# Softmax blocks transposed as they are: normalising attention outputs by row sums, and joining the two maps of differential attention, in a two-layer step

## The chip, the core and the metric

The kernel runs on one core of a Trainium2 chip. The metric is the device time of one execution in microseconds (us); less is better. TensorE is PE in the profile (its weight loads are PEld), VectorE is DVE, ScalarE is ACT, GpSimd is POOL, and SyncE, which issues many of the DMAs, is SP.

## What is computed

One inference step of a two-layer backbone on 128 prompt tokens and 512 sample tokens, model width 1024. Layer 0 mixes tokens by grouped-query attention (A, 8 heads) and by retention (B); layer 1 by differential attention (C, 4 heads, two maps each, values 128 wide) and by windowed attention (D, 8 heads, with a sink logit). After each mixer comes a channel mixer with 16384 single-neuron experts. The lines that matter here, shortened:

```python
# A and the prompt's D: softmax over keys, then the values
s = einsum('bhgqd,bhkd->bhgqk', qb, k) * scale        # D puts a sink logit in front
p = softmax(s, axis=-1)
o = einsum('bhgqk,bhkd->bhgqd', p, v)
# C: two softmax maps, one subtracted from the other
p = softmax(einsum('bhcqd,bhckd->bhcqk', qb, k) * d ** -0.5, axis=-1)
a = p[:, :, 0] - lam * p[:, :, 1]
o = einsum('bhqk,bhkv->bhqv', a, v)
c_out = rmsnorm(o, subln) * (1.0 - lam_init)
# D on sample tokens: sink, 128 context keys and a band |i-j| <= 128
p = softmax(concatenate([s_sink, s_ctx, s_band], axis=-1), axis=-1)
```

## The kernel before, in words

The activations lie transposed, features on the partitions and tokens along the free axis. The queries are taken in blocks of 128. For the sample tokens there are 640 keys (128 context, 512 own) in A and C, and three or four key blocks of 128 in D. The sample stream works in halves of two query blocks (`halves`, L756).

One softmax block is `soft_block` (L698): PE writes scores to a PSUM bank of tag `S`, DVE takes the row maximum (L713) and scales it to a bias (L716), ACT takes the exponential into the SBUF tile `P` with its row sum `rs` (L722), and DVE takes the reciprocal (L730). `win_block` (L1063) is the same for the windowed blocks, with the sink added to the sum (L1090) and the reciprocal at L1092. `P` has two buffers.

The value product needs the probabilities with keys on the partitions. Before, PE transposes and normalises at once: `diag` (L733) has DVE multiply the 128x128 identity by the reciprocals, the matrix `dg`, and `pT` (L742) multiplies each 128x128 block of `P` by `dg` in an ordinary matmul. For C (`attn_c`, L982) there are two such matrices, the second also multiplied by minus lambda (L739), and the two products add up in PSUM, so that the join of the maps costs PE two matmuls in each block. D does the same at L1037 and L1038. ACT then copies the result to SBUF (`PT`) and PE multiplies it by the values (L777, L1003, L1051, L1058).

```python
P, r = self.soft_block(...)                       # L771
self.pT([(P, self.diag(r))], nkt, pt[...])        # L772
nc.tensor.matmul(T[:, ...], P[:, o:o + 128], dg, start=i == 0, stop=i == len(parts) - 1)   # L752
```

The transposes of other tiles go through `transpose` (L316), a PE transpose against the identity. `head_bcast` (L488) spreads a per-token column over the partitions, one small matmul for each 128 tokens and head half.

What sets the order: `weave` (L235) interleaves the sample mixer with the prompt stream, with the weights of layer 1's modulation, and with the gather task (`gather_tile`, L1276). That task brings expert rows of 128x1024 by indirect DMA on POOL's queue (L1291) into eight buffers, and DVE works each up in one instruction (L1304 or L1308). The yields in the generators carry costs, and a scheduler then places every instruction on its engine by times that it reckons itself; each engine works in the order so made. PSUM in the mixers is four tags: `mm` and `S` with two buffers each, `tr` and `acc` with one. The projections (`chunk`, L554, matmuls at L474) write to `mm`, and so do rotary permutations (L501), broadcasts and the second half of `pT`. The prompt's layer 1 runs beside layer 0's dense experts, where every bank it takes is one bank, `pm`.

## Time and profile before

| | |
|---|---|
| time, median of 3 runs (range) | 4066.35 us (4053.7 to 4073.78) |
| the profiled execution's own time | 4054.7 us |
| its span in the trace | 4052.9 us |
| PE busy | 3686.1 us (91%) |
| PE weight loads busy | 3096.5 us (76%) |
| DVE busy | 3258.2 us (80%) |
| ACT busy | 1643.5 us (41%) |
| POOL busy | 1572.4 us (39%) |

Read it as an average over stages. The sample mixer of layer 0 lies at 305 to 608 us, that of layer 1 at 2255 to 2585 us; the rest is routing and dense experts, which the change does not touch. The share of an engine over the whole span says little about these two stretches, so they are read by themselves. A PE instruction's duration in the trace covers its way through the array; instructions follow one another faster than they last, so the cost of one in a row is the length of a run of them divided by their number.

### The profile page before, as it was taken

To read this page: it belongs to the slowest core of one execution; us is meant where nothing else is said; L and a number is where in the kernel's file an instruction comes from. 1 tells how busy PE (TensorE), PEld (TensorE's weight loads), DVE (VectorE), ACT (ScalarE), POOL (GpSimd) and SP (SyncE) were. 2 spreads that over 40 slices of the span, in tenths; PEclk is the share of its full clock that TensorE was granted. 3 is DMA by queue.
4 is the path that set the end of the run, shared out by engine and by line. 5 is a ranking of instruction groups with operands and counts; after the bars stand their busy time and mean duration, and the time that the engine had idled before them with its cause. 6 is when DMAs were issued, how large, how long until landed. Compare 5 with 4: busy or idle time off the path is not lost. (4 is left out here: it accounts for less than half of the span.)

```text
span 4052.9 us, 57181 instructions
## 1 busy us (share of the span) xinstructions
PE 3686.1 (91%) x19986; PEld 3096.5 (76%) x19986; DVE 3258.2 (80%) x6546; ACT 1643.5 (41%) x2971; POOL 1572.4 (39%) x1136
## 2 busy tenths in 40 slices
PE   7889888989985999999998888988977989999998
PEld 3775555889974887889886666677977878888887
DVE  3248788999998766878898888899999867777777
ACT  3223333335676333433333333333376743333333
POOL 1004655221344343433455666532142233443442
PEclk9999999999985999999998999999988989999999
DMA  8556887766878888999898677776677899998996
GB/s 324 175 176 231 320 293 274 247 230 214 286 261 306 307 325 328 349 338 352 305 315 288 238 241 257 246 249 234 215 257 246 290 341 322 342 331 302 317 312 217
DMA packets 441024, 1134.89 MB, mean 280 GB/s; under 512 B 40608, under 2 KB 191312, under 8 KB 434464
## 3 DMA queue, kind: packets, MB, share of 16 engines
q0 software_dynamic: 147904, 537.26, 37.9%
q1 hardware_dynamic: 251408, 506.28, 35.5%
q10 hardware_dynamic: 41424, 87.71, 5.9%
q8 instruction: 157, 2.57, 0.2%
q14 instruction: 131, 1.07, 0.1%
HBM read 1045.10 MB, written 85.98 MB: 279 GB/s over the span
## 5 line engine op out<-in xcount | busy, mean ns | idle before, releaser
L1291 POOL DMA_INDIRECT row<-v,xi x512 | 772.5, 1509 | 1218.9 <-DVE acc L1308 837.8
L1291 POOL DMA_INDIRECT row<-u,xi x512 | 690.8, 1349 | 793.0 <-DVE row L1304 566.5
L1400 PE MATMUL mm<-hhi,uhi 128*128 128x384 f32 x2048 | 702.4, 343 | 31.6 <-ACT uhi L1388 31.5
L1400 PE MATMUL mm<-hhi,ulo 128*128 128x384 f32 x2048 | 702.0, 344 | 27.2 <-DVE ulo L1389 27.1
L1400 PE MATMUL mm<-hlo,uhi 128*128 128x384 f32 x2048 | 697.5, 341 | 0.9 <-DVE hlo L448 0.9
L1304 DVE SCALAR_TENSOR_TENSOR row<-hn,row 128x1024 f32<-128x1024 f32 x512 | 629.2, 1255 | 27.5 <-DMA row<-u,xi 19.5
L1308 DVE SCALAR_TENSOR_TENSOR acc<-row,gw,acc 128x1024 f32<-128x1024 f32 x508 | 648.1, 1276 | 2.1
L1388 ACT CAST uhi<-u 128x1024 fp32r<-128x1024 f32 x256 | 269.7, 1053 | 535.8 <-PE mm L1400 241.3
L1423 PE MATMUL d<-vlo,Whi 128*128 128x512 f32 x1536 | 481.6, 394 | 2.1 <-DVE vlo L1464 2.0
L1423 PE MATMUL d<-vhi,Wlo 128*128 128x512 f32 x1536 | 476.4, 391 | 0.0
L1423 PE MATMUL d<-vhi,Whi 128*128 128x512 f32 x1536 | 433.3, 395 | 3.3 <-ACT vhi L1463 3.2
L1389 DVE TENSOR_TENSOR ulo<-u,uhi 128x1024 fp32r<-128x1024 f32 x256 | 311.7, 1217 | 153.8 <-ACT uhi L1388 150.8
L1400 PEld LDWEIGHTS mm<-hhi,uhi 128*128 128x128 f32 x2048 | 392.9, 192 | 45.0 <-ACT uhi L1388 38.4
L1400 PEld LDWEIGHTS mm<-hhi,ulo 128*128 128x128 f32 x2048 | 392.2, 192 | 38.6 <-DVE ulo L1389 35.4
L1400 PEld LDWEIGHTS mm<-hlo,uhi 128*128 128x128 f32 x2048 | 391.6, 191 | 6.8 <-DVE hlo L448 1.3
L1423 PEld LDWEIGHTS d<-vhi,Wlo 128*128 128x128 f32 x1536 | 288.6, 188 | 61.5
L1423 PEld LDWEIGHTS d<-vhi,Whi 128*128 128x128 f32 x1536 | 285.9, 189 | 58.5 <-ACT vhi L1463 4.7
L1423 PEld LDWEIGHTS d<-vlo,Whi 128*128 128x128 f32 x1536 | 285.8, 188 | 57.9 <-DVE vlo L1464 3.7
L1464 DVE TENSOR_TENSOR vlo<-v,vhi 128x1024 fp32r<-128x1024 f32 x256 | 311.3, 1217 | 20.2 <-ACT vhi L1463 20.1
L1471 ACT CAST Whi<-W 128x384 fp32r<-128x384 f32 x256 | 131.1, 513 | 392.8 <-PE d L1423 284.5
L1463 ACT CAST vhi<-v 128x1024 fp32r<-128x1024 f32 x256 | 268.7, 1050 | 49.3 <-DMA v<-v 32.6
L474 PE MATMUL mm<-hhi,whi 128*128 128x512 f32 x624 | 254.0, 408 | 20.5 <-ACT whi L463 6.5
(460 smaller groups left out, 6025.2 us busy)
## 6 DMA issues: line engine op xcount, KB each, us to landing
u<-ut SPq DMA_DIRECT2D x256, 512.0 KB, 5.1
v<-v SPq DMA_DIRECT2D x256, 512.0 KB, 5.9
Gd<-gst ACTq DMA_DIRECT2D x48, 1024.0 KB, 7.6
G<-Gd SPq DMA_DIRECT2D x64, 768.0 KB, 8.6
w<-win SPq DMA_DIRECT2D x80, 512.0 KB, 5.2
w<-wq SPq DMA_DIRECT2D x64, 512.0 KB, 4.7
Ad<-gpre ACTq DMA_DIRECT2D x152, 192.0 KB, 3.6
pre<-Ad SPq DMA_DIRECT2D x152, 192.0 KB, 6.1
```

Of the source, the lines that this page charges most:

```text
L474: nc.tensor.matmul(ps[:, :st.T], wp[a][:, k], h[b][:, k], start=(n == 0), stop=(n == 23))
L1291: nc.gpsimd.indirect_dma_start(out=r, out_offset=None, in_=self.A[f"{'uv'[n // 128]}{l}"], in_offset=bass.IndirectOffsetOnAxis(ap=xi[:, s: ...
L1304: nc.vector.scalar_tensor_tensor(r, hn, 1.0, r, op0=ALU.mult, op1=ALU.mult, accum_out=a[:, s:s + 1])
L1308: nc.vector.scalar_tensor_tensor(acc, r, w[:, s:s + 1], acc, op0=ALU.mult, op1=ALU.add)
L1388: nc.scalar.copy(hi, u)
L1389: nc.vector.tensor_tensor(lo, u, hi, op=ALU.subtract)
L1400: nc.tensor.matmul(ps[:, :ND], u[a][:, k], h[b][:, k, :ND], start=n == 0, stop=n == 23)
L1423: nc.tensor.matmul(acc[t][hf], a[:, ts], b[:, hf * 512:(hf + 1) * 512], start=(i == 0 and n == 0), stop=(i == 127 and n == 2))
L1463: nc.scalar.copy(vhi, v)
L1464: nc.vector.tensor_tensor(vlo, v, vhi, op=ALU.subtract)
L1471: nc.scalar.copy(whi, w)
```

## The change

Nothing is divided before the transpose any more. `soft_block` and `win_block` write the reciprocal into a column that the caller gives; `diag` is gone; `pT` and the code in D transpose `P` itself by `transpose`. In A and D the reciprocals of a chunk of two heads are gathered in a tile `ra`, and after the value product `normalise` spreads them by `head_bcast` into a `mm` bank (8 small matmuls for the sample, 2 for the prompt) and has DVE multiply the chunk of the output. In C the two unnormalised maps are joined on DVE: a factor `f` = (row sum 0) x (reciprocal 1) x (minus lambda), then P0 + f x P1 over the whole row; one transpose per block is left. The remaining factor, the reciprocal of row sum 0 (`cr`), is put into the root mean square that follows: the sums of squares are multiplied twice by `cr`, and the result once.

```diff
-    def soft_block(self, lhsT, rhs, nk, masks=None, sink=None, scale=0.125):
+    def soft_block(self, lhsT, rhs, nk, rout, masks=None, sink=None, scale=0.125):
...
-        r = self.wk.tile([128, 1], F32, tag="rr", name="rr", bufs=6)
-        nc.vector.reciprocal(r, rs)
-        return P, r
-
-    def diag(self, r, extra=None):
...
+        nc.vector.reciprocal(rout, rs)
+        return P, rs
+
+    def normalise(self, st, y, ra):
+
+        pb = self.bank("mm")
+        self.head_bcast(pb, ra, 0, st, 2)
+        self.nc.vector.tensor_tensor(y, y, pb[:, :st.T], op=ALU.mult)
...
-                for i, (P, dg) in enumerate(parts):
-                    nc.tensor.matmul(T[:, j * 128:(j + 1) * 128], P[:, o:o + 128], dg,
-                                     start=i == 0, stop=i == len(parts) - 1)
+                self.transpose(T[:, j * 128:(j + 1) * 128], P[:, o:o + 128])
...
         nc.scalar.copy(st.mo[:, cch], O[:, :st.T])
+        self.normalise(st, st.mo[:, cch], ra)
...
                 if cc == 3:
+                    for _ in range(2):
+                        nc.vector.tensor_tensor(st.hv, st.hv, st.cr, op=ALU.mult)
                     r = self.rsq(st.hv, 4 * st.nt)
+                    nc.vector.tensor_tensor(r, r, st.cr, op=ALU.mult)
...
-                    self.pT([(P0, self.diag(r0)), (P1, self.diag(r1, c["nlam"]))], nkt, pt[:, :, n * 128:(n + 1) * 128])
+                P0, s0 = self.soft_block(qs, st.ck[:, 0], st.nk, st.cr[:, hd * st.nt + i:hd * st.nt + i + 1])
+                r1 = self.wk.tile([128, 1], F32, tag="rr", name="rr", bufs=6)
+                P1, _ = self.soft_block(qs, st.ck[:, 1], st.nk, r1)
+
+                f = self.wk.tile([128, 1], F32, tag="rf", name="rf", bufs=6)
+                nc.vector.tensor_scalar(f, s0, r1, c["nlam"], op0=ALU.mult, op1=ALU.mult)
+                nc.vector.scalar_tensor_tensor(P0, P1, f, P0, op0=ALU.mult, op1=ALU.add)
+                self.pT(P0, nkt, pt[:, :, n * 128:(n + 1) * 128])
...
-                        nc.tensor.matmul(T2[:, jj * 128:(jj + 1) * 128], P[:, jj * 128:(jj + 1) * 128], dg,
-                                         start=True, stop=True)
+                        self.transpose(T2[:, jj * 128:(jj + 1) * 128], P[:, jj * 128:(jj + 1) * 128])
...
         nc.scalar.copy(st.mo[:, 4 + cch], O[:, :T])
+        self.normalise(st, st.mo[:, 4 + cch], ra)
```

Counted over the whole program, PE loses 456 matmuls against `dg` (320 of them on the sample in layer 0's A and layer 1's C counted with both maps, 112 in the sample's D, 24 on the prompt) and gains 372 transposes and 80 broadcast matmuls. An ordinary matmul of this type shows in the trace as two PE instructions, a transpose as one. DVE loses 120 products with the identity and gains 20 joins, 20 factors, 16 output products and 6 small products.

The order moves too, since the scheduler places instructions anew. Three places follow.

DVE, layer 1, sample, one query block of C (`mx` is the row maximum, `nm` the bias, `rr` and `cr` reciprocals, `row` a gathered expert row). Before:

```order
L713 TENSOR_REDUCE mx<-S 128x1 x2
L716 TENSOR_SCALAR nm<-mx 128x1 x2
L730 RECIPROCAL rr<-rs 128x1
L737 TENSOR_SCALAR dg<-c_ident,rr 128x128
L730 RECIPROCAL rr<-rs 128x1
L739 TENSOR_SCALAR dg<-c_ident,rr,lams 128x128
L1304 SCALAR_TENSOR_TENSOR row,ga<-hn,row 128x1024 x2
```

and with the change:

```order
L711 TENSOR_REDUCE mx<-S 128x1 x2
L714 TENSOR_SCALAR nm<-mx 128x1 x2
L727 RECIPROCAL cr<-rs 128x1
L727 RECIPROCAL rr<-rs 128x1
L1001 TENSOR_SCALAR rf<-rs,rr,lams 128x1
L1002 SCALAR_TENSOR_TENSOR P<-P,rf 128x640
L1308 SCALAR_TENSOR_TENSOR row,ga<-hn,row 128x1024 x2
```

The place of the two small matrices is taken by a factor and a product over 640 columns; the same two gathered rows follow.

PE, the same part of the program (`S` scores, `tr` and `mm` the banks of the transposes, `PTc` the transposed block, `cvs` the values). Before:

```order
L704 MATMUL S<-cks,cqs 128x320 x2
L752 MATMUL tr<-dg,P 128x128
L752 MATMUL mm<-dg,P 128x128
L704 MATMUL S<-cks,cqs 128x320 x2
L752 MATMUL tr<-dg,P 128x128 x5
L752 MATMUL mm<-dg,P 128x128 x3
L1003 MATMUL acc<-PTc,cvs 128x256 x5
```

and with the change:

```order
L702 MATMUL S<-cks,cqs 128x320 x4
L316 MATMUL tr<-c_ident,P 128x128 x3
L316 MATMUL mm<-c_ident,P 128x128 x2
L1007 MATMUL acc<-PTc,cvs 128x256 x5
```

Ten products for a query block become five transposes, and the scores of both maps of the next block stand ahead of them.

PE, layer 1, sample, the end of one head's D (`PTd` is D's transposed block, `vs` its values, `vsb`, `whi` and `hhi` belong to the projections of the next head, `ra` are the gathered reciprocals). Before:

```order
L1038 MATMUL tr<-dg,P 128x128 x3
L474 MATMUL mm<-hhi,whi 128x512
L474 MATMUL mm<-hlo,whi 128x512
L474 MATMUL mm<-hhi,wlo 128x512
L474 MATMUL mm<-hhi,whi 128x512
L474 MATMUL mm<-hlo,whi 128x512
L474 MATMUL mm<-hhi,wlo 128x512
L318 MATMUL mm<-c_ident,vsb 128x128 x4
L704 MATMUL S<-cks,cqs 128x320 x4
L1051 MATMUL acc<-PTd,vs 64x256
L1058 MATMUL acc<-PTd,vs 64x128
```

and with the change:

```order
L492 MATMUL mm<-c_ident,ra 64x128 x2
L1055 MATMUL acc<-PTd,vs 64x256
L1062 MATMUL acc<-PTd,vs 64x128
L316 MATMUL tr<-c_ident,P 128x128 x4
L1062 MATMUL acc<-PTd,vs 64x256 x2
L316 MATMUL tr<-c_ident,P 128x128 x3
L492 MATMUL mm<-c_ident,ra 64x128
L1055 MATMUL acc<-PTd,vs 64x256
L1062 MATMUL acc<-PTd,vs 64x128
L1062 MATMUL acc<-PTd,vs 64x256 x2
L499 MATMUL mm<-y,c_perm 128x512
L472 MATMUL mm<-hhi,whi 128x512
```

Before, all 96 projection matmuls of the next head stand between D's blocks, and the next head's first scores ahead of its last product. With the change 48 of the 96 and the rotary permutation stand behind D. The first broadcast of `ra` stands near D's beginning, so its `mm` bank is taken until the product on DVE at the chunk's end. It is so at each of the three changes of head.

## Rows read from the trace of the kernel before

**Rows 1.** Busy time by stretch, us (instructions), then clock, DMA share, GB/s.

```profile
core 0: us, PE busy (x) PEld busy (x) DVE busy (x) ACT busy (x) POOL busy (x), PEclk, DMA share, GB/s
305.00:608.00 303.00, 271.40 (x1752) 169.65 (x1751) 246.61 (x530) 101.72 (x202) 166.10 (x128) 0.97 0.79 282
2255.00:2431.00 176.00, 155.55 (x797) 120.32 (x796) 152.61 (x310) 60.04 (x151) 116.78 (x91) 0.95 0.72 238
2431.00:2520.00 89.00, 75.71 (x394) 57.98 (x393) 76.52 (x158) 32.15 (x81) 59.08 (x45) 0.98 0.71 238
2520.00:2585.00 65.00, 59.08 (x356) 48.07 (x354) 51.83 (x105) 30.35 (x76) 31.14 (x27) 1.00 0.70 242
```

**Rows 2.** Groups at 305 to 608 us: busy us, mean ns, idle before.

```profile
L752 PE MATMUL tr<-dg,P 128*128 128x128 f32 x192 | 28.9, 287 | 2.3 <-DVE dg L737 2.1
L752 PE MATMUL mm<-dg,P 128*128 128x128 f32 x128 | 20.3, 285 | 5.9 <-ACT rks L600 4.4 <-ACT PT L754 1.4
L737 DVE TENSOR_SCALAR dg<-c_ident,rr 128x128 f32<-128x128 f32 x32 | 10.9, 342 | 1.3 <-DVE rr L730 0.5
```

**Rows 3.** The same view at 2255 to 2585 us.

```profile
L1038 PE MATMUL tr<-dg,P 128*128 128x128 f32 x224 | 31.5, 281 | 0.0
L752 PE MATMUL tr<-dg,P 128*128 128x128 f32 x192 | 27.4, 280 | 0.0
L737 DVE TENSOR_SCALAR dg<-c_ident,rr 128x128 f32<-128x128 f32 x48 | 15.8, 329 | 3.1 <-DVE rr L730 0.5
L739 DVE TENSOR_SCALAR dg<-c_ident,rr,lams 128x128 f32<-128x128 f32 x16 | 6.1, 379 | 1.4
L945 DVE TENSOR_TENSOR xs<-xs,mm 128x512 f32<-128x512 f32 x4 | 2.7, 685 | 0.4 <-PE mm L494 0.4
```

**Rows 4.** Chain of waits, 2255 to 2590 us: start us, us, what.

```profile
2442.08 1.34 PE S L704 x4
...
2444.95 1.11 PE tr L752 x10
...
2446.73 2.32 PE acc L1003 x10
...
2554.34 1.98 PE mm L494 x16
...
2568.86 4.66 PE mm L474 x20
```

**Rows 5.** DVE in order of time, one query block of C: start us, us, instruction.

```profile
2447.39 0.27 DVE L716 TENSOR_SCALAR nm<-mx 128x1 f32<-128x1 f32 x2
...
2449.32 0.16 DVE L730 RECIPROCAL rr<-rs 128x1 f32<-128x1 f32 x1 [0.22 <-ACT P L722]
2449.60 0.35 DVE L739 TENSOR_SCALAR dg<-c_ident,rr,lams 128x128 f32<-128x128 f32 x1
2449.86 1.22 DVE L1304 SCALAR_TENSOR_TENSOR row<-hn,row 128x1024 f32<-128x1024 f32 x1
...
2453.61 0.27 DVE L716 TENSOR_SCALAR nm<-mx 128x1 f32<-128x1 f32 x2
```

**Rows 6.** PE in order of time around 24 transposes at 2178 us.

```profile
2178.53 2.78 PE L318 MATMUL d<-c_ident,dout 128*128 128x128 f32 x24
2186.35 1.11 PE L318 MATMUL pm<-c_ident,acc 128*128 128x128 f32 x4 [5.04 <-DVE acc L1308]
```

**Rows 7.** One DVE line's durations, ns min/median/max: a product and sum in SBUF.

```profile
L808 DVE SCALAR_TENSOR_TENSOR D<-c_delta,lg,D x16: 335/1092/1146, 34.9 to 542.7; 128x896 f32<-128x896 f32 x8, 128x128 f32<-128x128 f32 x8
```

**Rows 8.** DVE in order of time: a gathered row beside a POOL product.

```profile
2437.20 2.28 DVE L1304 SCALAR_TENSOR_TENSOR row<-hn,row 128x1024 f32<-128x1024 f32 x1
```

**Rows 9.** Busy time by stretch around the transposes of rows 6, columns as in rows 1.

```profile
2178.20:2181.20 3.00, 3.00 (x27) 2.73 (x25) 2.62 (x7) 1.51 (x4) 2.35 (x4) 1.00 0.84 281
2181.20:2184.20 3.00, 0.11 (x1) 0.00 (x0) 3.00 (x11) 0.00 (x0) 2.71 (x5) 1.00 0.95 311
2184.20:2201.20 17.00, 8.89 (x32) 3.80 (x32) 12.97 (x30) 7.75 (x12) 3.33 (x4) 0.50 0.94 323
```

More of the change, by code (lines that the diff above doesn't have):

```diff
@@ L762, in attn_a @@
         nkt = st.nk // 128
+        ra = self.inv_sums(st)
         O = self.bank("acc")
@@ L991, in attn_c @@
                 qs = st.cq[:, i * 128:(i + 1) * 128]
[L992 to L999 removed]
+                if hd == 0 and i == 0:
+                    st.cr = self.wk.tile([128, 4 * st.nt], F32, tag="cr" + st.name, name="cr", bufs=1)
+                P0, s0 = self.soft_block(qs, st.ck[:, 0], st.nk, st.cr[:, hd * st.nt + i:hd * st.nt + i + 1])
[5 more added lines that the diff above has]
+                self.pT(P0, nkt, pt[:, :, n * 128:(n + 1) * 128])
                 yield 4.3 if st.sample else 1.6
@@ L1027, in attn_d @@
                     qs = st.dq[:, i * 128:(i + 1) * 128]
+                    r = ra[:, 2 * i + g:2 * i + g + 1]
                     if not st.sample:
-                        P, r = self.soft_block(qs, st.kz[g], 128, sink=head)
-                        self.pT([(P, self.diag(r))], 1, pt)
+                        P, _ = self.soft_block(qs, st.kz[g], 128, r, sink=head)
+                        self.pT(P, 1, pt)
                         yield 0.9
                         continue
-                    P, r, blocks = self.win_block(st, qs, g, i, head)
+                    P, blocks = self.win_block(st, qs, g, i, head, r)
                     nb = len(blocks)
                     T2 = self.bank("tr")
-                    dg = self.diag(r)
                     for jj in range(nb):
-                        nc.tensor.matmul(T2[:, jj * 128:(jj + 1) * 128], P[:, jj * 128:(jj + 1) * 128], dg,
-                                         start=True, stop=True)
+                        self.transpose(T2[:, jj * 128:(jj + 1) * 128], P[:, jj * 128:(jj + 1) * 128])
                     ns = slice(n * 128, (n + 1) * 128)
@@ L1060, in attn_d, with win_block @@
         nc.scalar.copy(st.mo[:, 4 + cch], O[:, :T])
+        self.normalise(st, st.mo[:, 4 + cch], ra)
         yield 3.0 if st.sample else 0.3
-    def win_block(self, st, qs, g, i, head):
+    def win_block(self, st, qs, g, i, head, r):
         nc, c = self.nc, self.c
@@ L1090, in win_block @@
         nc.vector.tensor_tensor(rs2, rs, es, op=ALU.add)
-        r = self.wk.tile([128, 1], F32, tag="rr", name="rr", bufs=6)
         nc.vector.reciprocal(r, rs2)
-        return P, r, blocks
+        return P, blocks
     def peer_q(self, l, st):
```

26 lines of the change are left out of this document (7 added, 19 removed).

## The prediction

> **What bounds the kernel now.** I began with the busy times by stretch, because the whole-span shares mix the two mixers with dense stages that the change leaves alone. In layer 0's sample mixer PE is busy 271.40 of 303.00 us and DVE 246.61; in layer 1's three pieces PE is busy 155.55 + 75.71 + 59.08 = 290.3 of 330 us and DVE 152.61 + 76.52 + 51.83 = 281.0 [rows 1]. The reader is to see that layer 0 leans on PE and that in layer 1 the two engines are nearly level; in its middle piece DVE is even ahead, 76.52 to 75.71. So what PE is spared is worth most in layer 0, and in layer 1 only as long as DVE isn't made later.
>
> Second come the groups by line, for what the change touches. Products with `dg` cost PE 192 + 128 instructions in layer 0, and PE waited 2.1 us in all for `dg` [rows 2]. In layer 1 there are 224 for D and 320 for C (192 on `tr` as in the row shown, 128 on `mm`), and PE waited for none [rows 3].
>
> Third, the chain of waits gives lengths of runs, which are prices: ten `dg` instructions in 1.11 us, 0.111 each, and a matmul is two of them; sixteen broadcast instructions in 1.98 us, 0.124 each; twenty projection matmuls in 4.66 us, 0.233 each [rows 4].
>
> Last, DVE in order of time through one query block of C. From one bias to the next are 2453.61 − 2447.39 = 6.22 us, and after the second reciprocal at 2449.32 DVE goes from instruction to instruction: `dg` 0.28 us later, a gathered row 0.26 us after that, and so on to the next maxima [rows 5]. Its only slack lies ahead of that reciprocal, in the wait for ACT's exponentials. PE's part of such a block is two score groups of 1.34, 20 `dg` instructions (2.22) and half of a value group of 2.32 for two blocks [rows 4]: about 6.1 us. Both engines are near binding here, DVE a little more.
>
> **The change, part by part.** The sum is made against the profiled execution: 4054.7 us, of which 4052.9 are span. It lies 11.65 us under the median of the runs, 4066.35, so at the end I put the difference on the median.
>
> *Price of a transpose.* The trace has 24 PE transposes in a run of 2.78 us at a granted clock of 1.00 [rows 6, 9]; without the last one's way through the array, some 0.28 as a `dg` instruction's mean [rows 2, 3], that is 2.50 / 23 = 0.109 us each, one instruction in place of two. Four at half clock take 1.11 [rows 6], at most 0.28 each; that is the upper bound.
>
> *Layer 0, A.* PE loses 320 × 0.111 = 35.5 us, gains 160 × 0.109 = 17.4 and 64 broadcast instructions × 0.124 = 7.9: −10.2. DVE loses 32 matrices of 0.342 = 10.9 [rows 2] and gains four output products; the nearest row, 128x512 with one input in PSUM, has 0.685 [rows 3], so 2.7: −8.2. Both engines get shorter, so nothing takes over at once. PE is busy 90% of the stretch [rows 1], so I pass on 0.9 of it, −9.1, and most of the 2.1 us of waits for `dg`, since a transpose needs only `P`: **−11 us**. It is nothing if the stretch is held by the gathered rows or their DMAs (share 0.79 [rows 1]), and −12.3 at most.
>
> *Layer 1, C.* PE loses 35.5 us and gains 80 × 0.109 = 8.7: −26.8 over 16 blocks, 1.7 each. But DVE sets the pace. In the block above, the first `dg` lay in the wait for the second exponential, so its removal shortens nothing; the second one's 0.26 us go. After the second reciprocal come the factor and the join, and the same two gathered rows behind them. No row shows a join of 128x640. The same form takes 0.335 us at 128x128 and 1.092 at 128x896 [rows 7]; on the line between them 640 columns come to 0.84. The factor lies between a reciprocal's 0.16 and a matrix's 0.28 of pace [rows 5]; I take 0.2. So 0.84 + 0.2 − 0.26, about **+0.8 us for each block**. Bounds: with 0.335 for the join +0.3; stretched as a gathered row is beside a POOL product (2.28 us [rows 8] against 1.22 [rows 5]), 1.57 and so +1.5. Twelve blocks lie beside D of the head before: 12 × 0.8 = 9.6. In the last head PE is busy 59.08 of 65.00 us [rows 1] and its relief pays part of the delay; for its four blocks I take half, 1.6. Together **+11 us**, between +5 and +24. PE's saving vanishes into waits for DVE.
>
> *Layer 1, D.* PE: 224 × 0.111 = 24.9 lost, 112 × 0.109 = 12.2 and 7.9 for broadcasts gained: −4.8. DVE: 32 matrices × 0.329 = 10.5 lost [rows 3], 4 × 0.685 = 2.7 and a few short products of the root mean square gained: about −7. The lesser of the two passes: **−5 us**.
>
> *The projections behind D.* At three changes of head 48 projection matmuls stand behind D instead of inside it: 48 × 0.233 = 11.2 us each. I cost this at nothing, since DVE keeps some ten gathered rows of 1.22 us for that place [rows 5], and C's first blocks of the next head wait for both. Without that cover it is rival B.
>
> *The rest.* ACT's copies `PT` keep their number and size. On the prompt PE loses 24 matmuls (48 × 0.111 = 5.3), gains 20 transposes (2.2) and 32 broadcast instructions (4.0): +0.9, beside routing and dense work; DVE loses as much as it gains. Nothing.
>
> Sum: −11 + 11 − 5 = **−5 us**, 4049.7 for an execution like the profiled one, and 4066.35 − 5 = **4061 us** on the median. With the bounds of A and C alone it goes from −12.3 + 5 − 5 = −12 to 0 + 24 − 5 = +19, that is 4054 to 4085.
>
> **The rivals.**
>
> *A: PE sets the end in both stretches.* Then the scheduler's new order lets DVE run its gathered rows elsewhere, and C's ring isn't what counts. PE saves 10.2 + 2.1 in layer 0 and 26.8 + 4.8 in layer 1, 43.9; at its busy shares of 0.90 and 0.88 that is some −39 us: 4027. For it speak 271.40 of 303.00 and 290.3 of 330 [rows 1]. Against it: in C, DVE has no gap between the second reciprocal and the next bias [rows 5], and its gathered rows fill layer 1 to 281.0 of 330.
>
> *B: the bank of the broadcasts holds the projections up.* The first broadcast of `ra` near D's beginning takes one of two `mm` banks until DVE's product at D's end, so half of the next head's projections come late. It decides if DVE is through with its rows before PE is through with the 48. Then 3 × 11.2 = +33.6, with −5 for the rest +28.6: 4095, slower. For it speaks the order; against it, that DVE is as full as PE there.
>
> *C: PE's clock falls.* The 24 transposes ran at a granted 1.00, 2.4 GHz, and the clock stood at 0.50, 1.2 GHz, after 3 us in which PE did 0.11 us of work; there the transposes come in a group of four in a stretch with PE busy 8.89 of 17.00 us [rows 9]. So a gap went before the fall, and the change makes gaps: PE's block in C shrinks to two scores of 1.34, five transposes (0.55) and 1.16 of values, 4.4 us out of 7.0. At half clock that is 8.8, 1.8 above DVE's ring, × 16 = +29; with the sum 4066 − 5 + 29 = 4090, slower. Against it: scores and values stand between the transposes, and no gap as long as that one is in sight. The Trainium skill, "TensorE: Matmul & The Clock Gate", section "Part 4: PE-mode transpose", states that a transpose doesn't count as busy for the clock gate in the way that a matmul does, which speaks against this change. By that rule C's transposes would count with the gaps and this rival would be the likely one; the trace agrees only in so far as the clock fell just after a run of transposes, and the empty 3 us explain that as well.
>
> *D: transposes cost PE what the products with `dg` did*, two passes each, 0.222. Then PE gains 80 × 0.222 only in C, and loses broadcasts; DVE's part stays. Layer 0: +7.9 × 0.9 − 2 = +5; C +11; D +8: +24 in all, 4090 at the most, and less where DVE's relief covers the broadcasts. The row of 24 transposes speaks against it [rows 6].
>
> **How the numbers follow.** My forecast has 0.56, A 0.24, B 0.08, C 0.06, D 0.06. The whole effect is small because the relief of PE in C has no taker; that is the weakest step, hence 0.24 for A. About 20 us (0.5%) is what a measurement of this kernel can tell from no change. A and 0.06 from the forecast's lower side make faster 0.30. B, half of C (0.03) and a third of D (0.02) make slower 0.13. The rest, 0.50 + 0.03 + 0.04, is the same, 0.57. The range goes from 4024, just past A's 4027, to 4090, past the forecast's own 4085: outside are about 0.10 of A below, B's 0.08 and some of C above.
>
> **What would show it.** In the profile after, 320 instructions on `tr` and `mm` in A and C become transposes with 0.109 us of pace; if it is 0.22, D holds. From bias to bias in C should be about 7.0 us, with factor and join between reciprocal and row and PE waiting for DVE; if it is 6.2 or less, A is near. The stretch of layer 0 should shorten by about 11 us and that of layer 1 grow by about 6. At the changes of head DVE should still be at its rows when the 48 projections run; if it waits there and PE doesn't, B holds. A granted clock near 0.5 in C would be C. The prediction is wrong if layer 1 gets shorter by 20 us or more, or longer by 25.

## The result and the profile after

The change is slower: 4111.78 us against 4066.89 us (medians of 4 runs each), a ratio of 1.0107 with a 95% interval of 1.0085 to 1.0129. Forecast were 4061 us with a range of 4024 to 4090, so both the sign and the range were wrong. The profiled execution took 4102.43 us with a span of 4100.7.

First the busy line of the page after the change: PE has 380 instructions less than before, and still only 4.4 us less to do.

```profile
PE 3681.7 (90%) x19606; PEld 3064.9 (75%) x19606; DVE 3252.6 (79%) x6488; ACT 1637.1 (40%) x2970; POOL 1539.8 (38%) x1136
```

Then the busy times by stretch after the change, layer 0's sample mixer and layer 1's three pieces, cut where the work of [rows 1] begins and ends (columns as there):

```profile
305.60:612.00 306.40, 270.04 (x1644) 160.45 (x1642) 242.99 (x505) 100.42 (x202) 162.85 (x129) 0.93 0.79 280
2273.50:2463.30 189.80, 149.72 (x652) 105.90 (x650) 150.41 (x295) 59.44 (x151) 114.70 (x92) 0.90 0.67 223
2463.30:2558.40 95.10, 74.43 (x319) 53.47 (x320) 76.74 (x152) 30.89 (x80) 57.38 (x45) 0.88 0.66 221
2558.40:2626.50 68.10, 57.09 (x285) 42.18 (x285) 54.06 (x102) 30.38 (x77) 27.05 (x26) 0.91 0.62 212
```

Layer 0 takes 306.4 us against 303, the pieces of layer 1 take 189.8, 95.1 and 68.1 against 176, 89 and 65: 23 us more. DVE has as much to do there as before (281.2 us against 281.0), so it is idle for 23 us more. The granted clock of PE fell in all four.

Two marks measure the places better than a cut by eye. One is the row of C's bias on the sample, whose first and last start enclose most of layer 1's mixer. The groups of that line, before and after:

```profile
L716 DVE TENSOR_SCALAR nm<-mx x32: 135/142/154, 2264.7 to 2538.6; 128x1 f32<-128x1 f32 x32
```

```profile
L714 DVE TENSOR_SCALAR nm<-mx x32: 131/143/155, 2285.9 to 2581.8; 128x1 f32<-128x1 f32 x32
```

From first to last that is 273.9 us before and 295.9 after, **22.0 more**. The other mark is the first and last product of layer 0's dense experts with their values, beside which the prompt's layer 1 is woven (last two numbers ahead of the semicolon), before and after:

```profile
L1423 PE MATMUL d<-vhi,Whi x768: 387/389/793, 1316.0 to 2175.6; 128*128 128x512 f32 x192
```

```profile
L1427 PE MATMUL d<-vhi,Whi x768: 387/390/794, 1323.6 to 2204.3; 128*128 128x512 f32 x192
```

These products take 859.6 us before and 880.7 after, 21 more; some of it is given back on the way to C, and from the first product to C's first bias it is 2264.7 − 1316.0 = 948.7 against 2285.9 − 1323.6 = 962.3, **13.6 more**. The rest of the 47.8 us between the two spans is 7.6 ahead of the dense experts and 4.5 behind C. Both lie within the scatter of one order: the first dense product starts between 1316.0 and 1333.4 us in the eight profiles of this case whose order up to there is that of before, and behind C the second profile of the old order differs by 6.

The ring in C, from one bias to the next, came out as forecast. DVE in order of time through one block of C after the change, from bias to bias:

```profile
2480.97 0.27 DVE L714 TENSOR_SCALAR nm<-mx 128x1 f32<-128x1 f32 x2
2482.13 0.16 DVE L727 RECIPROCAL cr<-rs 128x1 f32<-128x1 f32 x1 [0.88 <-ACT P L720]
2482.90 0.16 DVE L727 RECIPROCAL rr<-rs 128x1 f32<-128x1 f32 x1 [0.61 <-ACT P L720]
2483.10 0.27 DVE L1001 TENSOR_SCALAR rf<-rs,rr,lams 128x1 f32<-128x1 f32 x1
2483.41 0.89 DVE L1002 SCALAR_TENSOR_TENSOR P<-P,rf 128x640 f32<-128x640 f32 x1
2484.21 1.22 DVE L1308 SCALAR_TENSOR_TENSOR row<-hn,row 128x1024 f32<-128x1024 f32 x1
...
2487.97 0.27 DVE L714 TENSOR_SCALAR nm<-mx 128x1 f32<-128x1 f32 x2
```

2487.97 − 2480.97 = 7.00 us, where [rows 5] had 6.22: factor and join stand between the second reciprocal and the row, and DVE has no slack behind them. PE's part got cheap as forecast: five transposes of a block, PE in order of time, stand 0.11 us apart (three from 2478.87 to 2479.20).

```profile
2478.87 0.49 PE L316 MATMUL tr<-c_ident,P 128*128 128x128 f32 x3
2479.20 0.38 PE L316 MATMUL mm<-c_ident,P 128*128 128x128 f32 x2
```

What PE is spared it waits: from C's first to last bias it is idle for 61 us, against 32 before. The longest of these waits is ahead of C's scores, until ACT has read the last ones out of the bank, 33.5 us against 22.8; and ACT reads them only with DVE's bias.

### The profile page after: what moved, and what is told of

It is laid out like the page before. It is cut to its first block, busy times and chain, and to the rows that moved or that the text cites. A ratio compares the mean times of both kernels' runs of the same rounds, so it can differ in the third digit from the quotient of the medians.

```text
span 4100.7 us, 56359 instructions
## 1 busy us (share of the span) xinstructions
PE 3681.7 (90%) x19606; PEld 3064.9 (75%) x19606; DVE 3252.6 (79%) x6488; ACT 1637.1 (40%) x2970; POOL 1539.8 (38%) x1136
## 5 line engine op out<-in xcount | busy, mean ns | idle before, releaser
L1295 POOL DMA_INDIRECT row<-v,xi x512 | 753.4, 1472 | 1219.6 <-DVE acc L1312 849.3
L1295 POOL DMA_INDIRECT row<-u,xi x512 | 676.8, 1322 | 830.2 <-DVE row L1308 608.5
L1427 PEld LDWEIGHTS d<-vhi,Whi 128*128 128x128 f32 x1536 | 287.2, 190 | 64.5 <-ACT vhi L1467 10.8
```

The source lines that it names most:

```text
L1295: nc.gpsimd.indirect_dma_start(out=r, out_offset=None, in_=self.A[f"{'uv'[n // 128]}{l}"], in_offset=bass.IndirectOffsetOnAxis(ap=xi[:, s: ...
L1427: nc.tensor.matmul(acc[t][hf], a[:, ts], b[:, hf * 512:(hf + 1) * 512], start=(i == 0 and n == 0), stop=(i == 127 and n == 2))
```

## The experiments

Ratios are to runs of the kernel before on the same chip, which stood at 4069 to 4072 us in the different calls. "Layer 1" below is the time from C's first to last bias, 273.9 us before.

### Which part costs what

Each part was first taken out of the change, then put alone into the kernel before. The edit is of the same kind everywhere: the part's blocks go back to `diag` and products with `dg`, with no broadcast, output product or join, for instance in D (`new` is false for a part in the old form):

```diff
+                    dg = None if new else self.diag(r)
                     for jj in range(nb):
+                        if not new:
+                            nc.tensor.matmul(T2[:, jj * 128:(jj + 1) * 128], P[:, jj * 128:(jj + 1) * 128], dg,
+                                             start=True, stop=True)
+                            continue
                         self.transpose(T2[:, jj * 128:(jj + 1) * 128], P[:, jj * 128:(jj + 1) * 128])
```

A part taken out is taken out on the sample and on the prompt, a part put in alone only on the sample.

C put back:

> Only C goes back to diagonal matrices (no join, no factor); A, D and the prompt's A and D stay changed. Both theories expect the ring from bias to bias in C to go back from 6.98 to 6.2 us, 12 x 0.77 = 9 us. Theory 1 expects the clock in C to come back as well, so layer 1 shorter by 15 to 22 us, total near 4092; theory 2 expects the 9 us and no more, 4103, since D's broadcasts still hold a bank and 48 projections still stand behind D.

4081.06 us, ratio 1.0038 (1.0022 to 1.0053), 31 us less than the full change. Its bias in C and its dense products:

```profile
L714 DVE TENSOR_SCALAR nm<-mx x32: 135/142/155, 2273.3 to 2556.0; 128x1 f32<-128x1 f32 x32
```

```profile
L1462 PE MATMUL d<-vhi,Whi x768: 387/389/795, 1327.3 to 2190.3; 128*128 128x512 f32 x192
```

Layer 1 takes 282.7 us, 13 less than with the full change. Another 16 lie ahead of it: from the first dense product to C it is 2273.3 − 1327.3 = 946.0 against 962.3. The sample's C has no part there; the prompt's C has lost its join there, and the order is another. So C on the sample accounts for 13 of the 31 us, not for all.

A put back:

> Only A goes back to diagonal matrices. If the change in A was a gain of about 11 us by itself that something else ate, the time rises to some 4120; if A's transposes cost what they spare (layer 0 came out 3 to 4 us longer after the change, and the clock fell there for 44 us against 17), the time falls by 3 to 8 us, to 4104 to 4109.

4098.07 us, ratio 1.0069 (1.0042 to 1.0095), 14 us less than the full change. The gain isn't in layer 0. It lies in the dense stretch, where A's code has no part and the new code of the prompt's layer 1 is untouched; the dense products of this kernel:

```profile
L1458 PE MATMUL d<-vhi,Whi x768: 387/389/793, 1323.1 to 2181.7; 128*128 128x512 f32 x192
```

That is 858.6 us, with the same PE instructions, but for some two dozen of 4350, that took 880.7 in the full change, in another order; from the first of them to C it is 949.0 us against 962.3. The busy times between first and last product (columns as in [rows 1]), before, with the full change, and with A put back:

```profile
1316.00:2175.60 859.60, 841.08 (x4350) 738.15 (x4349) 692.87 (x1145) 328.21 (x516) 367.26 (x252) 0.99 0.92 329
```

```profile
1323.60:2204.30 880.70, 849.99 (x4356) 739.47 (x4354) 703.36 (x1158) 326.75 (x515) 352.72 (x258) 0.98 0.90 325
```

```profile
1323.10:2181.70 858.60, 840.54 (x4346) 736.21 (x4345) 692.07 (x1144) 328.45 (x516) 348.79 (x252) 0.99 0.92 329
```

In the full change's order PE is idle for 30.7 us there, against 18.5 before and 18.1 with A put back, and it is busy for 9 us more at a slightly lower clock.

D put back:

> Only D goes back to diagonal matrices, sample and prompt. Theory 2 (the broadcasts of D hold a bank of the projections): the 48 projections move back inside D, layer 1 shortens by 10 us or more, 4100 or less. Theory 1 (clock): D's products add PE work that holds the clock, 5 to 10 us as well, but the order of the projections decides nothing. If D's part was the gain of 5 us forecast, the time rises to 4117.

4111.39 us, ratio 1.0114 (1.0087 to 1.0142): no change. With D's broadcasts gone nothing holds the second `mm` bank, all 96 projections stand inside D again, and layer 1 is no shorter (301.3 us). So rival B, the bank, isn't what makes this kernel slow; what it costs by itself shows in D alone, below.

The prompt put back, all its parts:

> The change on the sample tokens; on the prompt all blocks go back to diagonal matrices. Between layer 0's routing and layer 1's mixer (the prompt's layer 1 beside dense experts) the change came out 12 us longer. If the prompt's new chain (joins, broadcasts and products through one bank) costs that, the time falls by 8 to 16 us, to 4096 to 4104; if those 12 us are only an order that happened to fall badly, the time stays near 4112 or falls as much for another reason, and the waits of PE for the prompt's blocks tell which.

4091.79 us, ratio 1.0054 (1.0036 to 1.0071), 20 us less. The dense products take 2180.7 − 1322.1 = 858.6 us as in the kernel with A put back, while layer 1 stays at 297.4:

```profile
L1478 PE MATMUL d<-vhi,Whi x768: 387/389/774, 1322.1 to 2180.7; 128*128 128x512 f32 x192
```

Two different edits remove the same stretch's loss, one of which leaves the prompt's code in it alone. So the prompt's new operations cost little by themselves (949.0 us to C with them and A in the old form, 945.8 to 949.4 in the order of before); the order in which the scheduler put them between the dense products did. In the four profiles that have the full change's order there the products take 880.7 to 881.6 us, in eight with the order of before 856.8 to 860.1. Four other orders, of kernels that differ from the full change in one part, lie between, at 862.3 to 867.5. Which exchange in the order costs it stays open.

Now each part alone in the kernel before. A on the sample:

> The kernel before with A's sample blocks alone in the new form; C, D and the whole prompt as before. The forecast gave this part 11 us of gain. Layer 0's mixer in the profile of the full change was 3 us longer than in the one profile of before and its clock fell for 48 us against 20, so my theory is now that the gain is mostly given back: 0 to 5 us faster than before. The rival, that A's gain is real and something else ate it: 8 to 12 us faster.

4064.08 us, ratio 0.9984 (0.9968 to 1.0000): a gain of 0 to 13 us, most likely 7. Its profile doesn't show that gain in layer 0, where the change in A is. From the first to the last bias of A on the sample it takes 291.5 us; nine profiles with A in the old form have 281.2 to 292.6 there, ten with transposes 281.8 to 293.6, in the mean 288.0 and 287.7. It is the stretch from the first dense product to C that is shorter, 940.3 us against 945.8 to 949.4 in the order of before: again another order of instructions that the edit didn't touch.

D on the sample:

> The kernel before with D's sample blocks alone in the new form. Forecast of this part: 5 us of gain. With C put back, layer 1 was still 10 us longer than before, with 4 us more of DVE idle time between the C blocks of two heads; so I expect D alone to be 5 to 12 us slower than before. If it is within 3 us of before, those 10 us belong to the prompt or to the profile's own scatter.

4077.13 us, ratio 1.0019 (1.0005 to 1.0034): 2 to 14 us slower, layer 1 at 2551.2 − 2268.5 = 282.7 us. The three stretches from the last bias of one head of C to the first of the next, where D lies, take 64.3, 64.5 and 67.3 us against 62.1, 62.0 and 64.6, 7.4 more. DVE's waits for the output product there (us in total, times, longest):

```profile
DVE xs L763 <- ACT xs L1114: 7.7, 3, 2.7
```

PE in turn waits 4.2 us for that product, which frees the bank. That is rival B's mechanism in small: 48 projections of each head stand behind D here as in the full change, and 7.4 us are lost, not 33.6. DVE's wait is about as long as the loss; the new place of the projections came with it, and the two weren't separated. With C put back the stretches have the same order and 195.5 us in sum, as here (196.1).

C on the sample:

> The kernel before with C's sample blocks alone in the new form (factor and join on DVE); the prompt as before. Forecast of this part: +11 us, all of it in the ring of 16 blocks. With D put back the layer was 30 us longer, with C put back 10, so I expect +11 in the ring and 5 to 12 more in the stretches between the heads: 15 to 25 us slower than before. If it is 9 to 12 us, the ring is all.

4107.5 us, ratio 1.0080 (1.0058 to 1.0103): 33 us slower, more than expected. Layer 1 takes 306.9 us. First to last bias of each head's blocks are 24.6, 23.7, 23.3 and 25.1 us against 22.6, 21.2, 21.2 and 20.3, together 11.4 more, the ring as forecast. The three stretches from the last bias of one head to the first of the next are 71.3, 68.3 and 70.6 us against 62.1, 62.0 and 64.6: **21.5 more**, where this kernel's D is the old one. The first of these, last and first bias, before and here:

```profile
2287.12 0.27 DVE L716 TENSOR_SCALAR nm<-mx 128x1 f32<-128x1 f32 x2
...
2349.30 0.20 DVE L716 TENSOR_SCALAR nm<-mx 128x1 f32<-128x1 f32 x2
```

```profile
2307.17 0.27 DVE L714 TENSOR_SCALAR nm<-mx 128x1 f32<-128x1 f32 x2
...
2378.59 0.19 DVE L714 TENSOR_SCALAR nm<-mx 128x1 f32<-128x1 f32 x2
```

All parts back, a second profile of the old order:

> All parts in the old form: the instructions and their order on each engine are those of the kernel before. A second profile of the same program: its span, the lengths of the stages and the time at half clock tell how far two profiles of one order lie apart. From the runs' range of 20 us I expect the span up to 15 us above 4052.9, spread over the stages, and the clock in the mixers within 15 us of the first profile's 20 and 20 us at half.

Span 4060.1, layer 1 at 274.0 and the dense products at 857.4. What lies ahead of the dense experts (1319.9) and behind C (1520.2 against 1514.3) differs by 4 and 6 us between two executions of one order; layer 1 differs by 0.1. So a difference of several us in layer 1 is read from one profile below, and one of 6 us in the rest isn't; the 0.1 rests on two profiles, and pieces of layer 1 differ by up to 1.1 us between them.

### The clock

Rival C says that PE's clock is what costs. The Trainium skill ("TensorE: Matmul & The Clock Gate", "Part 4: PE-mode transpose"), by which a transpose doesn't count as busy for the clock gate as a matmul does, would make it likely. The trace of the next run agrees in direction (in layer 1's mixer 75 us at half clock, 1.2 GHz, with transposes, 51 with matmuls in their place), but PE had more work there too, so no run here shows that rule by itself. Each block of `P` turned by an ordinary product with the identity, here and at the same place in D:

```diff
-                self.transpose(T[:, j * 128:(j + 1) * 128], P[:, o:o + 128])
+                nc.tensor.matmul(T[:, j * 128:(j + 1) * 128], P[:, o:o + 128], self.c["ident"], start=True, stop=True)
```

> The change, but each block of P is turned by an ordinary matmul against the identity (two PE instructions of 0.111 us) instead of a transpose (one of 0.109 us); broadcasts, join and output products stay. PE gets 372 x 0.11 = 41 us more work, the other engines none. Theory 1 (PE's clock: in layer 1's mixer the clock stood at 1.2 GHz for about 72 us after the change, against 20 before, because transposes leave PE with less of the work that holds the clock): the half-clock time in the two mixers falls back towards that of before, and the time falls by 10 to 25 us, to 4087 to 4102. Theory 2 (the new order: the DVE ring in C of 6.98 us, the projections behind D, and gaps in PE, set the time and the clock only follows the gaps): the time stays within 5 us of 4112 or rises by up to 15.

4132.38 us, ratio 1.0162 (1.0139 to 1.0186), 20 us slower than the change. The half-clock time in layer 1's mixer fell from 75 to 51 us, and the time rose all the same. The order moved too, so a second run kept the transposes and issued C's score products twice:

```diff
-            for i in range(2):
+            for i in list(range(2)) * (2 if twice else 1):
                 nc.tensor.matmul(S[:, i * 512:i * 512 + n2], lhsT, rhs[:, i * n2:(i + 1) * n2], start=True, stop=True)
```

> The change, with each of the sample's score matmuls in C issued twice (16 blocks x 8 more instructions of 0.30 us at full clock, 39 us of PE work that computes nothing new); DVE, ACT and POOL have the same work, and the order is that of the change up to layer 1's mixer. It fills the holes in PE that C's ring leaves. Theory 1 (the fallen clock in layer 1 is what costs): half-clock time in layer 1's mixer falls from 75 us to below 40 and the time falls by 8 to 20 us, to 4092 to 4104, although PE does more. Theory 2 (DVE's ring with the join, and waits behind it): the ring stays at 6.98 us, the time within 5 us of 4112, or up to 15 more.

4107.59 us, ratio 1.0095 (1.0071 to 1.0119), the same as the change within its scatter. From C's first to last bias, busy times and clock (columns as in [rows 1]), of the change and of this kernel:

```profile
2285.90:2581.80 295.90, 234.82 (x1007) 167.77 (x1008) 237.72 (x468) 98.25 (x249) 174.89 (x138) 0.89 0.68 227
```

```profile
2285.80:2582.50 296.70, 251.23 (x1123) 179.39 (x1123) 239.06 (x469) 97.28 (x248) 180.13 (x141) 0.96 0.68 229
```

The clock goes from 0.89 to 0.96, as high as the same stretch had in the two profiles of the old order (0.96 and 0.95), and the length doesn't move (295.9 and 296.7 us). So the fallen clock isn't the cause of the loss in layer 1. For the dense stretch, where time at half clock rose from 17 to 31 us, no run tests it.

### What in C costs

The join taken from DVE in two ways. By GpSimd:

```diff
-                nc.vector.scalar_tensor_tensor(P0, P1, f, P0, op0=ALU.mult, op1=ALU.add)
+                if st.sample:
+                    nc.gpsimd.tensor_scalar(P1, P1, f, None, op0=ALU.mult)
+                    nc.gpsimd.tensor_tensor(P0, P0, P1, op=ALU.add)
+                else:
+                    nc.vector.scalar_tensor_tensor(P0, P1, f, P0, op0=ALU.mult, op1=ALU.add)
```

> The change, with the join of C's maps on the sample done by GpSimd as a product and a sum of 128x640 (some 1.4 us each by a product of 128x512) instead of by DVE. Theory 2 expects the ring of C at about 6.1 us (6.98 less the join's 0.8), 12 x 0.8 = 10 us and more where the waits behind it go too: 4090 to 4102. If POOL's products delay its gathers of expert rows, or stretch DVE's rows beside them to 2.3 us, it is nothing, or up to 20 us slower. Theory 1 expects no gain, since PE does the same.

4155.65 us, ratio 1.0198 (1.0177 to 1.0220), the worst of all. The groups of POOL in layer 1 tell why:

```profile
L1003 POOL TENSOR_SCALAR P<-P,rf 128x640 f32<-128x640 f32 x16 | 52.2, 3262 | 11.4 <-DVE rf L1001 10.1 <-ACT es L1097 1.2
L1004 POOL TENSOR_TENSOR P<-P 128x640 f32<-128x640 f32 x15 | 23.9, 1591 | 1.2
```

The product takes 3.26 us there and the sum 1.59, against 0.95 for both on DVE, and POOL issues the gathers. A head's blocks now take 27.8 to 29.3 us.

By PE, which joins in PSUM as before, with one matrix instead of two:

```diff
-                nc.vector.tensor_scalar(f, s0, r1, c["nlam"], op0=ALU.mult, op1=ALU.mult)
-                nc.vector.scalar_tensor_tensor(P0, P1, f, P0, op0=ALU.mult, op1=ALU.add)
-                self.pT(P0, nkt, pt[:, :, n * 128:(n + 1) * 128])
+                nc.vector.tensor_scalar(f, s0, c["nlam"], None, op0=ALU.mult)
...
+                nc.vector.tensor_scalar(dg, c["ident"], r1, f, op0=ALU.mult, op1=ALU.mult)
+                self.pT2([(P0, c["ident"]), (P1, dg)], nkt, pt[:, :, n * 128:(n + 1) * 128])
```

> The change in A and D; in C the first map is turned against the identity and the second against a matrix of identity x 1/(row sum 1) x (-lambda x row sum 0), added up in PSUM as before, so the join goes back to PE, one of two matrices per block goes, and the root mean square still carries the rest. Ring of C about 6.2 us as before the change. Theory 2: near the kernel with C put back (4081), 4075 to 4088. Theory 1: the same or a little lower, since PE has the same work as there.

4082.15 us, ratio 1.0035 (1.0017 to 1.0053), like C put back; layer 1 at 282.7 us. So the moved division isn't what costs in C: the join on DVE, with what goes with it in the order, costs 13 us in layer 1. The other 16 us lie ahead of C as with C put back (946.4 us from the first dense product), where the prompt's join is gone as well.

Next the two halves of C's change apart. The join without PE's relief:

```diff
+                    if st.sample:
...
+                        nc.vector.tensor_scalar(f, s0, r1, 0.0, op0=ALU.mult, op1=ALU.mult)
+                        nc.vector.scalar_tensor_tensor(P0, P1, f, P0, op0=ALU.mult, op1=ALU.add)
                     self.pTd([(P0, self.diag(r0)), (P1, self.diag(r1, c["nlam"]))], nkt, pt[:, :, n * 128:(n + 1) * 128])
```

> The kernel before, with a factor of zero and a join P0 + 0 x P1 added on DVE in each of the sample's C blocks; both diagonal matrices and PE's ten products for a block stay. DVE in the ring gets 0.28 + 0.80 us more, PE is relieved of nothing. If C's loss (36 us with C's sample blocks alone in the new form) is DVE's longer ring and what the order makes of it, this is as bad: 25 to 45 us slower than before. If it comes from the holes in PE and its clock, this is slower by the ring alone, 12 to 17 us.

4116.61 us, ratio 1.0124 (1.0096 to 1.0151), 50 us for 1.1 us more on DVE in each of 16 blocks. The heads' blocks take 114.2 us, 29 more than before, so DVE's own time isn't all. PE's waits say what else (us in total, times, longest):

```profile
PE tr L751 <- DVE P L1035: 33.6, 15, 4.0
```

The join stands ahead of PE's products in the block's chain. With the relief, in the full change, PE waits 0.7 us for it and the blocks take 96.3: beside the join, PE's relief isn't worthless. PE's relief without the join (the edit drops the lines of `f` and the join):

> C's sample blocks in the new form without factor and join: only the first map's probabilities are turned and used, and the second map's softmax is computed and left unused. PE has the relief of the new form, DVE has 0.26 us less for each block than before. If DVE's ring is the cause, the ring falls to about 5.96 us and the time to 4055 to 4070, no slower than before. If PE's holes and clock are the cause, it is 10 us or more slower than before although DVE does less.

4085.08 us, ratio 1.0032 (1.0017 to 1.0048). The time is what was expected for holes in PE and its clock, but that isn't where it goes: a head's blocks are shorter than before (21.7, 19.3, 20.4 and 19.6 us), though 33 of the 46 us at half clock lie in them. The busy times of its three stretches between the heads (columns as in [rows 1]) show where the loss in layer 1 lies:

```profile
2299.10:2368.50 69.40, 57.95 (x281) 43.35 (x281) 56.10 (x111) 21.01 (x56) 43.71 (x35) 0.95 0.68 223
2387.80:2448.90 61.10, 54.96 (x281) 41.61 (x281) 54.73 (x110) 21.22 (x56) 39.90 (x30) 1.00 0.73 227
2469.30:2537.90 68.60, 56.25 (x281) 42.57 (x281) 57.52 (x113) 22.66 (x59) 40.52 (x31) 0.95 0.63 208
```

The same PE instructions (281) and 27 gathered rows in each, the same program, and 69.4, 61.1, 68.6 us. What differs is the order that the scheduler gave them, and only the middle head has D's order of before. In this profile, the slowest of eight runs, layer 1 is 6 us longer than before and the part behind C 23, so it doesn't place all of the loss. So the order between the heads was the suspect, and it is set by a number: the yield behind a C block tells the weave how much other work goes with it.

```diff
-                yield 4.3 if st.sample else 1.6
+                yield 3.4 if st.sample else 1.6
```

In the kernel with C alone in the new form:

> C's sample blocks alone in the new form, with the yield behind a C block at 3.4 instead of 4.3, so that the order has two gathered rows in every block and the join ahead of D's first maximum where C hands over to D (with 4.3 that maximum stands ahead of the last join in two of three heads, and of three rows). If the 22 us lost between the heads are the order at this handover and after it, they fall by 8 us or more, to 4085 to 4100; if they follow from the longer ring in any order, the time stays at 4100 to 4115.

**4064.37 us, ratio 0.9995 (0.9973 to 1.0016): 34 us of loss are gone with one number**, join and all. The three stretches are back at 62.5, 61.0 and 64.9 us, and the blocks of the first three heads hold 6 gathered rows instead of 7, the stretches 26 instead of 27. The handover of a head's last block to D, DVE in order of time, first with 4.3:

```profile
2309.30 0.27 DVE L1042 TENSOR_SCALAR rf<-rs,rr,lams 128x1 f32<-128x1 f32 x1
2310.48 0.56 DVE L1137 TENSOR_REDUCE mx<-S 128x1 f32<-128x384 f32 x1 [0.91 <-PE S L1134]
2310.95 0.87 DVE L1043 SCALAR_TENSOR_TENSOR P<-P,rf 128x640 f32<-128x640 f32 x1
2311.75 1.22 DVE L1359 SCALAR_TENSOR_TENSOR row<-hn,row 128x1024 f32<-128x1024 f32 x1
...
2315.18 0.20 DVE L1139 TENSOR_SCALAR nm<-mx,nsink 128x1 f32<-128x1 f32 x1
```

and with 3.4:

```profile
2299.11 0.27 DVE L1042 TENSOR_SCALAR rf<-rs,rr,lams 128x1 f32<-128x1 f32 x1
2299.42 0.89 DVE L1043 SCALAR_TENSOR_TENSOR P<-P,rf 128x640 f32<-128x640 f32 x1
2300.22 1.22 DVE L1359 SCALAR_TENSOR_TENSOR row<-hn,row 128x1024 f32<-128x1024 f32 x1
...
2303.58 0.33 DVE L1139 TENSOR_SCALAR nm<-mx,nsink 128x1 f32<-128x1 f32 x2
```

With 4.3 DVE takes D's first maximum ahead of the last join and waits for its scores, which PE, in this place in its order, begins only after a hole, at half clock:

```profile
2308.39 0.77 PE L1125 MATMUL S<-kz0s,dqs 128*128 128x128 f32 x2 [3.91 <-issue]
```

From factor to D's first bias it is 5.88 us, against 4.47, and one more gathered row (1.15) is most of that. The larger loss follows behind it, in DVE's waits for gathered rows, from C's first to last bias: in the old order, with C alone at 4.3, and at 3.4 (us in total, times, longest).

```profile
DVE row L1359 <- DMA row<-u,xi: 5.0, 9, 1.5
```

```profile
DVE row L1359 <- DMA row<-u,xi: 22.4, 12, 4.3
```

```profile
DVE row L1359 <- DMA row<-u,xi: 10.4, 7, 3.0
```

Since POOL starts a gather only when DVE has freed one of eight buffers (after the change POOL waits 608.5 us in all for DVE's row line), a stall of DVE can delay the gathers that it will wait for next; this chain is argued, not shown. Nor are these waits the whole account, for the old kernel with 3.4, below, has 11.4 us of them and loses nothing. That the order decides is shown by the number alone; which single exchange in it does, the handover or the rows behind it, wasn't tried apart.

### The full change again, and what beats it

> The whole change with nothing but the yield behind a C block of the sample at 3.4 instead of 4.3. If the order between the heads is what made C cost 25 us beyond its ring, the time falls from 4112 by 15 to 30 us, to 4082 to 4097; the prompt's 12 to 15 us and D's 6 stay. If the order with D in its new form is as bad with any yield, it stays at 4105 or more.

4091.55 us, ratio 1.0038 (1.0025 to 1.0050): 20 us of the 45 come back, as expected. Layer 1 is 285.9 us, with the stretches between the heads at 195.3 in sum; the dense products still take 2212.5 − 1330.9 = 881.6.

> A and C of the sample in the new form with the yield behind a C block at 3.4; D and the prompt as before. A alone was 7 us faster than before, C alone with this yield 3 us faster within its scatter. If the parts add, 5 to 14 us faster than before, 4058 to 4067; if the order of one part undoes the other's, no faster.

4072.0 us, ratio 0.9998 (0.9989 to 1.0008): it is no faster than before, so A's 7 us don't come on top of C with 3.4.

> The kernel before with the yield at 3.4: what that number does by itself. If it only repairs the order that C's new form brought, this is within 8 us of before; if fewer gathered rows among the C blocks are better in any case, it is faster by as much as the short yield seems to give C.

4062.22 us, ratio 0.9976 (0.9961 to 0.9990): the old kernel gains 10 us by that number, with layer 1 at 2544.5 − 2272.8 = 271.7 us. So the number isn't only a repair of C, and no version in the new form that was tried is faster than the old kernel with it: compared at 3.4 the full change is still some 29 us slower. By the two profiles 18 of them lie between the first dense product and C (963.8 us against 945.8), 7 in C's blocks (90.6 against 83.4) and 7 in the stretches between the heads (195.3 against 188.4), 32 in sum. C alone at 3.4 is 8.0 us longer in layer 1 than the old kernel at 3.4, all of it in its blocks (91.3 against 83.4); its stretches are as long (188.4).

## Why the prediction was wrong

- **C's ring: right.** Forecast were +0.8 us for each block and 7.0 us from bias to bias; 0.78 and 7.00 were measured in the block shown, and +11.0 us over the four heads' blocks in the full change (24.6 + 23.3 + 23.3 + 25.1 = 96.3 against 85.3), where +11 was forecast. That the sums agree so well is partly luck: from first to last bias the first three heads grew by 6.2 over nine rings, where 0.8 each makes 7.2, and the last one, whose delay PE's relief was to halve, by 4.8 over three (3.7 against the second profile of the old order), where 0.4 each makes 1.2. The join's line has 0.95 us in the mean against 0.84 taken, the factor 0.27 against 0.2. That PE's relief finds no taker held without the join (81.0 us of blocks against 85.3, of which 12 × 0.26 = 3.1 is the matrix that DVE is spared); beside the join it pays for a part of it.
- **"The rest", put at "Nothing": the step that failed.** The prompt's layer 1 was to cost nothing beside the dense work, since its sums of work came out even. From the first dense product to C's first bias it became 13.6 us longer, and not for the prompt's operations: almost the same instructions in another order, with A put back, take 949.0 us, as before. That the dense stretch is one "which the change does not touch" doesn't hold; its instructions, the prompt's among them, got another order.
- **"Layer 1, D" at −5 and "the projections behind D" at "nothing": failed as well, wrong in sign.** The stretches between the heads became 66.3, 64.7 and 68.7 us, together 11.0 longer. About 7 of that is D's new form with the order that came with it: 7.4 with D alone, 6.8 with C put back, 6.9 when both kernels have 3.4. DVE did have less to do, but the output product was costed at its 0.685 us (0.69 measured) and not at its wait for ACT's copy of the output, 7.7 us in D alone and 3.4 in the full change; what the projections' new place costs beside that stays open. The other 4 came with C's new form, by the order: C alone at 4.3 makes them 21.5 longer, at 3.4, with every operation kept, no longer than in the old kernel, and in the full change the 4 are gone at 3.4 too (195.3).
- **A, −11: not there.** From A's first to last bias the profiles show 288.0 us in the mean with the old form and 287.7 with transposes. Alone A is worth 0 to 13 us, most likely 7, and its profile has that in the dense stretch. The forecast's own range for it was −12 to 0. Why layer 0 gives nothing back, with PE and DVE both relieved there, stays open.
- **The range.** It was made of the bounds of A and C alone; D and the rest stood in it without any. From the forecast's −5 to the 47.8 us between the two spans it is 52.8: 16.0 of it are D with the projections, 13.6 the rest, 11 A's gain that isn't there, and 12 the scatter ahead of the dense experts and behind C.
- **Rival B, the bank:** out as the main cause, by the run with D put back, and in D alone worth at most 7.4 us of its 33.6. **Rival C, the clock:** the clock did fall, to 0.89 in C, and the run with doubled scores gave it back without any time, so in layer 1 it isn't the cause. **Rival D:** out; three transposes stand 0.11 us apart. **Rival A:** out, the time rose and DVE sets the pace of C.
- The chance of slower, 0.13, came only from single mechanisms. That a scheduler redraws the order of some thousand instructions, and that this order can cost as much as the operations, wasn't among the rivals. By these runs it is the largest term, some 18 us of the 45: 13.6 beside the dense experts and about 4 between the heads. It goes both ways, for from the first dense product to C the kernels here take 940.3 to 963.8 us.

## What to carry to other kernels

Where a program orders the work from costs that it reckons itself, an edit has two prices: its instructions, and the new order. The first can be worked out from rows, as C's ring shows; the second can't, and it is worth one run of each part alone and one with the number that sets the weave, before an edit is judged. Moving work from an engine that waits (PE in C) to one that sets the pace (DVE) lengthened C's blocks by 11 us although both engines had less to do in all. And where a part is taken out, it is worth looking where in the trace the time came back: of 31 us that went with C, 16 weren't in its place.

## What the runs showed of the hardware

- The granted clock fell with PE's holes, with and without transposes: 0.89 in C's stretch with holes in every ring, 0.96 with the same transposes where scores issued twice fill them, and 0.91 with the join added to the old kernel, where no block of `P` is turned by a transpose and PE is idle for 63 us of 326. Whether a transpose holds the clock less than a matmul, these runs don't separate. That last stretch, columns as in [rows 1]:

```profile
2269.80:2596.10 326.30, 263.17 (x1264) 201.42 (x1264) 251.65 (x520) 98.62 (x247) 174.55 (x140) 0.91 0.63 207
```

- The clock scatters by itself. Layer 0's mixer in two profiles of the same instructions in the same order, all parts back and the old kernel with the short yield (which moves nothing before layer 1):

```profile
306.70:614.30 307.60, 274.64 (x1757) 170.72 (x1756) 248.99 (x533) 102.59 (x203) 166.43 (x129) 0.97 0.79 280
```

```profile
304.20:620.90 316.70, 284.36 (x1757) 178.07 (x1756) 246.49 (x533) 102.45 (x203) 163.44 (x129) 0.94 0.77 272
```

0.97 and 0.94, 307.6 and 316.7 us. So the fall from 0.97 to 0.93 in layer 0 after the change isn't evidence for a cause.
- A product of 128x640 with a per-token factor took 3.26 us on GpSimd (mean of 16), and product and sum in one instruction 0.95 us on DVE (mean of 16).
